# The gate of the residual folded into w_o on GpSimd, and the expert gathers taken from the unscaled rows

## The chip, the cores and the metric

One Trainium2 chip; the kernel runs on one of its cores. The time is the device time of one execution in microseconds (us). Before the change three executions took 749.11 us in the median (748.03 to 749.79). The engines: PE multiplies matrices (PEld is its loading of the stationary operand), DVE and ACT work on rows of 128 partitions, POOL is GpSimd, SP issues nearly all the transfers from HBM.

## The reference

One transformer layer on 256 tokens of 1024 channels in float32. What matters here is its second half:

```python
x = x + g1 * _mixer_out(...)          # _mixer_out ends in matmul(merged, w_o)
x = x + g2 * _hier_moe(_rmsnorm(x, norm2_g) * (1 + sc2) + sh2, ...)
# _hier_moe: top-1 of 4 groups, top-2 of the 8 experts in it, 32 experts of 1024 -> 512 -> 1024
for e in range(N_EXPERTS):
    hid = silu(t @ w1[e]) * (t @ w3[e])
    out = out + combine[:, e:e + 1] * (hid @ w2[e])
```

The gate `g1` is one number per output channel, so `g1 * (m @ w_o)` equals `m @ (w_o * g1)`. The root of `_rmsnorm` is one number per token.

## The kernel before

The mixer comes first, about 300 us. Each float32 weight is split on the way into a high part (ACT, `highs`) and the rest (DVE, `lows`, of the loaded tile `ld` and `highs`), half a tile (128x1024) at a time, and PE multiplies in three passes. PE, ACT and DVE work through a list written out by hand (`WORK`, lines 54 to 60): `s o 3` starts the split of half 3 of `w_o` on ACT, `l o 3` finishes it on DVE, `o k` and `N b k` are the matmuls of the output projection, `m` is a step of the modulation vectors on DVE (`macc`). While `run(WORK)` records, each of the three engines keeps the order of the list; POOL is outside of it and keeps the order in which its own instructions were scheduled.

Near the end of the list stand the steps that lead to the experts, for five pieces of the rows (`pieces2`): `ra` (line 1201) multiplies the product by the gate `gain(0)` on DVE, adds it to the row tile `xt()` and squares it on ACT; `rb` transposes on PE and copies on ACT; `rc` multiplies by the router weights; `rd` adds up sums of squares; `L t` makes the root of token tile `t` and its logits; `rt` chooses the experts; `pl` counts each token's place in its expert (`rank`). `rw` scales the rows by the root into a new tile `h2`, laid out as `(t, k, 128)`, and `ac` puts the rows into the accumulators `acc`.

After the list: `onehots(e)` (line 1301) compares places with slot numbers for four experts, so that `gather` (line 1316) can pull their tokens, transposed, by matmuls whose stationary operand is a 128x128 piece of `h2` and whose moving operand is the one-hot tile `oh`; DVE and ACT evict them with the modulation into `xg`. The experts go in 16 pairs: `hidden_mm` (line 1338) runs 8 rows `k` of w1 and w3 for two experts, `down` multiplies by w2, `scatter` adds into `acc`. For the first pair the second half of the gather stands at `k == 4` of `hidden_mm`.

The order of the transfers: about 20 buffers of 1 MB (lane `r`) hold weights. A planner (`plan_loads`) walks the recorded events of the program (a buffer taken, a buffer freed, a load first needed, a load done) and puts each load at the first event from which a buffer stays free. On the chip a load then waits in SP's queue until the last reader of the buffer it takes has ended. For the loads of this story: the buffers of the merged rows and of the splits are freed at step `hh` (line 1252), the buffer of the row tile at `done("x")` after the list, and the next ones by the first pair: `hidden_mm` declares its weights done after `k == 3` and after `k == 7`.

Of the kernel before, what the change touches and what calls it, by code (L numbers as in the profile page):

```python
# [10 lines left out]
I32 = mybir.dt.int32  # L11
# [118 lines left out]
def hybrid_block_kernel(  # L130
# [1005 lines left out]
    ss2 = sb(keep, [128, 2, 3], "ss2")  # L1136
    lg = sb(keep, [128, 2, 36], "lg")
# [99 lines left out]
    @step  # L1237
    def step_rd(p):
        t = pieces2[p][0]
        i = max(1, p - 2)  # L1240
        dve.tensor_tensor(out=ss2[:, t, 0:1], in0=ss2[:, t, 0:1], in1=ss2[:, t, i:i + 1], op=ALU.add)

    @step
    def step_L(t):

        r = banks["r2", t] = rstd_of(ss2[:, t, 0:1], D, f"rs2{t}")[0]
        dve.scalar_tensor_tensor(out=lg[:, t, :], in0=banks["lg", t][:, 0:36], scalar=r, in1=lb, op0=ALU.mult, op1=ALU.add)
        release(banks["lg", t])
# [8 lines left out]
    @step  # L1257
    def step_rw(t, n):

        act.activation(out=ready["h2"][:, t].rearrange("q k p -> q p k")[:, 64 * n:64 * n + 64],  # L1260
                       in_=xt()[:, t, 512 * n:512 * n + 512].rearrange("q (p k) -> q p k", k=KT), func=AF.Copy,
                       scale=banks["r2", t])
# [14 lines left out]
    rk_ps, h2 = banks["rk"], ready["h2"]  # L1277
# [3 lines left out]
    done("x")  # L1281
    for t in range(2):
        pe.matmul(rk_ps[0:1, 64:96], ones[:, 0:1], selm[:, t].rearrange("p g e -> p (g e)"), start=(t == 0), stop=(t == 1))
    cnt = sb(keep, [1, 1], "cnt")
    dve.tensor_reduce(out=cnt, in_=rk_ps[0:1, 64:96], axis=AX.X, op=ALU.max)
    cnt_i = sb(keep, [1, 1 + NE], "cnt_i", I32)
    dve.tensor_copy(out=cnt_i[:, 0:1], in_=cnt)
    dve.tensor_copy(out=cnt_i[:, 1:1 + NE], in_=rk_ps[0:1, 64:96])
    release(rk_ps)


    free_h, free_y = [free_m.pop(0)], [free_p.pop(0)]
    free_m.append(free_p.pop(0))
    while len(free_m) > 2:
        free_p.append(free_m.pop())
# [5 lines left out]
    def onehots(e):  # L1301
# [14 lines left out]
    def gather(kps=range(4), behind=None):  # L1316

        for kp in kps:
            ps = bank("xg_ps")
            pv = ps[:, 0:8 * CAP].rearrange("p (k n) -> p k n", k=2)  # L1320
# [6 lines left out]
            if kp % 2:  # L1327
                for kk in range(2):
                    act.activation(out=xg[:, kp, kk], in_=pv[:, kk], func=AF.Identity, scale=am2[:, 1, 2 * kp + kk:2 * kp + kk + 1],  # L1329
                                   bias=sh2[:, 1, 2 * kp + kk:2 * kp + kk + 1])  # L1330
            else:
                for kk in range(2):
                    k = 2 * kp + kk
                    mark["xg"] = dve.tensor_scalar(out=xg[:, kp, kk], in0=pv[:, kk], scalar1=am2[:, 1, k:k + 1],  # L1334
                                                   scalar2=sh2[:, 1, k:k + 1], op0=ALU.mult, op1=ALU.add)
# [87 lines left out]
    for p in range(NP):  # L1423
        hp = hidden_mm(lambda e, k: xg[:, k // 2, k % 2, CAP * (2 * (p % 2) + e):CAP * (2 * (p % 2) + e) + CAP],
                       *loaded_of(p), None if p else lambda: gather((2, 3)))
# [7 lines left out]
        if p % 2 and p + 1 < NP:  # L1433
# [7 lines left out]

    if events is not None:
# [60 lines left out]
    with tc.If(n_max > CAP):  # L1503
        for (t, n), a in acc.items():
            act.copy(out=xs[:, t, 512 * n:512 * n + 512], in_=a)
        with tc.For_i(0, NE, 1) as ei:
            n_own = nc.values_load(cnt_i[0:1, bass.ds(ei + 1, 1)], min_val=0, max_val=T)
            with tc.If(n_own > CAP):
# [136 lines left out]
```

## Time and profile before

| | before |
|---|---|
| median of three runs | 749.11 us (748.03 to 749.79) |
| the profiled execution | 747.63 us, its span 745.9 us |
| PE busy, DVE, ACT, POOL | 647.3, 289.4, 206.2, 9.9 us |
| moved from HBM | 265.66 MB read, 358 GB/s over the span |
| chain that ended last | DMA 51%, PE 45%, DVE 2%, ACT 1% |

The span has two parts. Up to about 310 us PE is busy nearly all the time and the chain of waits runs through it. From there the chain is the transfers of the experts' weights (192 MB), one after another, until 732 us. The row `PE 7999...` of the page shows the first part, `GB/s` (420 to 422 in nearly every slice of the second half) the second.

### The profile page before, as it was taken

Reading aid. Unit: us, or ns where it says so; the run is one execution under the profiler, and the core shown is the slowest. Engines: PE = TensorE matmul, PEld = TensorE weight load, DVE = VectorE, ACT = ScalarE, POOL = GpSimd, SP = SyncE. Lnnn points to the kernel's source line nnn. Section 1 sums busy time; section 2 is a strip of 40 time slices with the busy share of each in tenths; the row PEclk is TensorE's granted clock in tenths of the full one; section 3 lists DMA queues with packets and bytes.
Section 4 is the critical chain, followed back from the end, with each engine's and each line's share of the span. In section 5 each row is a group of like instructions: output and inputs, shape, how many; then the busy total and the mean of one; then the engine's idle time right before and its main releaser. Section 6 shows DMA issues by size and latency. Waiting matters only on the chain.

```text
span 745.9 us, 9959 instructions
## 1 busy us (share of the span) xinstructions
PE 647.3 (87%) x4050; PEld 367.8 (49%) x4051; DVE 289.4 (39%) x584; ACT 206.2 (28%) x387; POOL 9.9 (1%) x19
## 2 busy tenths in 40 slices
PE   7999999999999999899978867878977886887663
PEld 6789978879999988443313212222311321221110
DVE  4577986798676677421201200200200120020002
ACT  3345755786555566310000000000100000000012
POOL 0000000010000000000000000000000000000000
PEclk9999999999999999999989999989998999999997
DMA  9997542479998899999999999999999999999993
GB/s 319 362 397 302 196 151 71 133 271 365 350 352 296 322 339 345 360 422 421 420 422 421 421 422 420 420 422 421 421 420 422 421 421 422 420 421 422 420 421 146
DMA packets 55609, 267.43 MB, mean 359 GB/s; under 512 B 4612, under 2 KB 13572, under 8 KB 28804
## 3 DMA queue, kind: packets, MB, share of 16 engines
q1 hardware_dynamic: 54610, 266.19, 89.8%
q8 instruction: 34, 0.56, 0.3%
q10 hardware_dynamic: 948, 0.55, 0.2%
q14 instruction: 17, 0.14, 0.0%
HBM read 265.66 MB, written 1.05 MB: 358 GB/s over the span
## 4 chain that ended last, share of the span: by engine, by line
DMA 51%; PE 45%; DVE 2%; ACT 1%; issue 1%; SPq 0%; DVEq 0%; ACTq 0%
DMA ld<-in_moe_w_dram 50%; PE v L158 6%; PE hp L1347 4%; PE k L158 3%; PE Y L158 3%; PE wo L158 3%; PE g L158 2%; PE u L158 2%; PE q L158 2%; PE U L158 2%; PE V L158 2%; PE X L158 2%; PE T L158 2%; PE W L158 2%; PE G L158 1%; PE s_ps L158 1%
## 5 line engine op out<-in xcount | busy, mean ns | idle before, releaser
L1347 PE MATMUL hp<-ld,bc 128*32 128x512 f32 x1024 | 197.2, 641 | 47.0 <-DMA ld<-in_moe_w_dram 46.9
L1347 PEld LDWEIGHTS hp<-ld,bc 128*32 128x32 f32 x1024 | 40.9, 116 | 170.1 <-DMA ld<-in_moe_w_dram 90.9
L1381 PE MATMUL yp<-ld,wk 128*32 128x512 f32 x512 | 85.0, 600 | 18.1 <-DMA ld<-in_moe_w_dram 18.1
L1361 DVE COPY wk<-hp 128x256 f32<-128x256 f32 x16 | 6.7, 421 | 145.5 <-ACT wk L1360 145.5
L158 DVE TENSOR_TENSOR lows<-ld,highs 128x1024 fp32r<-128x1024 f32 x46 | 56.1, 1221 | 14.4 <-ACT highs L158 14.3
L158 ACT CAST highs<-ld 128x1024 fp32r<-128x1024 f32 x46 | 48.2, 1053 | 32.3 <-DMA ld<-in_w_in_dram 9.2
L1360 ACT COPY wk<-hp 128x256 f32<-128x256 f32 x16 | 5.9, 369 | 174.8 <-PE hp L1347 174.8
L1329 ACT ACTIVATE bc<-xg_ps,mcol 128x128 f32<-128x128 f32 x32 | 14.2, 457 | 125.1 <-PE hp L1347 114.2
L1381 PEld LDWEIGHTS yp<-ld,wk 128*32 128x32 f32 x512 | 17.2, 109 | 63.6 <-DMA ld<-in_moe_w_dram 39.0
L1323 PEld LDWEIGHTS xg_ps<-wr,h 128*128 128x128 f32 x256 | 31.4, 191 | 30.2 <-issue 26.0
L1334 DVE TENSOR_SCALAR bc<-xg_ps,mcol 128x128 f32<-128x128 f32 x32 | 12.8, 409 | 81.6 <-PE hp L1347 77.0
L1386 DVE TENSOR_TENSOR yb<-yp,bc 128x512 f32<-128x512 f32 x16 | 11.1, 692 | 82.9 <-PE yp L1381 82.9
L1403 PE MATMUL acc<-yb,wk 64*128 64x512 f32 x128 | 31.8, 615 | 11.1 <-DVE yb L1386 11.1
L158 DVE SCALAR_TENSOR_TENSOR macc<-ld,sj,macc 128x1024 f32<-128x1024 f32 x32 | 40.3, 1278 | 0.0
L1323 PE MATMUL xg_ps<-wr,h 128*128 128x128 f32 x256 | 38.6, 290 | 0.0
L1368 ACT ACTIVATE wk<-hT 128x256 f32<-128x256 f32 x16 | 6.2, 384 | 97.0 <-PE yp L1381 89.0
L1403 PEld LDWEIGHTS acc<-yb,wk 64*128 64x128 f32 x128 | 11.0, 186 | 32.3 <-DVE yb L1386 23.8
L158 ACT ACTIVATE gx<-gx 128x256 f32<-128x256 f32 (+2 forms) x56 | 24.8, 484 | 4.7 <-DVE gx L158 3.7
L158 PE MATMUL wo<-highs,ot 128*128 128x512 f32 (+1 forms) x80 | 20.0, 354 | 0.0
L158 PE MATMUL Y<-ot,highs 128*128 128x256 f32 x128 | 18.3, 285 | 0.0
L1312 DVE TENSOR_TENSOR yb<-cst,rank 128x128 f32<-128x128 f32 x32 | 9.0, 288 | 23.0 <-PE woT L1393 19.6
L1365 PE MATMUL hT<-cst,wk 128*128 128x128 f32 x64 | 12.9, 294 | 4.6 <-ACT wk L1360 4.0
(319 smaller groups left out, 913.0 us busy)
## 6 DMA issues: line engine op xcount, KB each, us to landing
ld<-in_moe_w_dram SPq DMA_DIRECT2D x191, 1024.0 KB, 19.8
ld<-in_w_mod_dram SPq DMA_DIRECT2D x24, 1024.0 KB, 5.3
ld<-in_w_in_dram SPq DMA_DIRECT2D x22, 1024.0 KB, 8.2
ld<-in_w_o_dram SPq DMA_DIRECT2D x4, 1024.0 KB, 8.4
ld<-in_w_gla_br_dram SPq DMA_DIRECT2D x4, 1024.0 KB, 10.1
ld<-in_w_pool_br_dram SPq DMA_DIRECT2D x2, 1024.0 KB
ld<-in_xT_dram SPq DMA_DIRECT2D x1, 1024.0 KB
ld<-in_cT_dram SPq DMA_DIRECT2D x1, 1024.0 KB
```

Source lines behind the costliest of these rows:

```text
L158: i = f(*args, **kwargs)
L1312: dve.tensor_tensor(out=wo, in0=slots_of[:, None, None, :].to_broadcast([128, 2, 2, CAP]), in1=rank[:, t, None, es, None].to_broadcast([12 ...
L1323: i = pe.matmul(pv[:, kk, :], h2[:, t, 2 * kp + kk, :], oh[:, t].rearrange("p e s -> p (e s)"), start=(t == 0), stop=(t == 1))
L1329: act.activation(out=xg[:, kp, kk], in_=pv[:, kk], func=AF.Identity, scale=am2[:, 1, 2 * kp + kk:2 * kp + kk + 1], bias=sh2[:, 1, 2 * kp + ...
L1334: mark["xg"] = dve.tensor_scalar(out=xg[:, kp, kk], in0=pv[:, kk], scalar1=am2[:, 1, k:k + 1], scalar2=sh2[:, 1, k:k + 1], op0=ALU.mult, o ...
L1347: mark["hp"] = pe.matmul(hp[o:o + CAP, :], xs(e, k), w[:, 512 * (k % 4):512 * (k % 4) + 512], start=(k == 0), stop=(k == KT - 1), tile_pos ...
L1361: dve.tensor_copy(out=hs[:, 2:4], in_=hv[:, 2:4])
L1365: pe.transpose(out=tp[:, 128 * k:128 * k + 128], in_=hs[:, k, :], identity=ident)
L1368: last_silu[:] = [act.activation(out=hid, in_=tv[:, :, 0, :], func=AF.Silu)]
L1381: pe.matmul(yp[r:r + CAP, :], hid[:, 2 * k + e, :], w[:, o:o + 512], start=(k == 0), stop=(k == 3), tile_position=(0, r))
L1386: dve.tensor_tensor(out=yb, in0=yp, in1=g2bc[:, 0:512], op=ALU.mult)
L1403: pe.matmul(acc[t, n], wT[rs, 128 * t:128 * t + 128], yb[rs, :], start=start, stop=stop, tile_position=(64 * n, 0))
```

## The change

The gate is multiplied into the halves of `w_o` on POOL, where `half_of` hands them to the split, in place; `ra` then adds the product straight to the rows. The sums of squares of both token tiles are reduced at once and one root is made for both. `rb` copies its last two pieces on DVE. There is no `h2`: `gather` reads the row tile itself, in steps of 8 elements (`xk`), and the root goes into the one-hots. The first gathers and their one-hots are made for two experts at a time, the second gather of the first pair stands at `k == 2`, and experts 2 and 3 are gathered after the first pair's `hidden_mm`. The row tile stays held to the end (`event("done", ...)`), so that buffer is not freed after the list; `h2` takes none.

```diff
-    N 2 4, ra 1, N 2 5, N 0 6, rb 0, N 0 7, sr 2, N 1 6, ra 2, N 1 7, N 2 6, rb 1, ra 3, N 2 7, rc 0, rb 2, rb 3, rc 1,
-    ra 4, rd 2, rd 4, rb 4, rc 2, rc 3, rc 4, hh, rd 3, ac 0 0, L 0, L 1, ac 1 0, ac 1 1, rt, rw 1 1, rw 0 0, pl,
-    ac 0 1, rw 0 1, rw 1 0"""
+    N 2 4, ra 1, N 2 5, N 0 6, rb 0, N 0 7, sr 2, N 1 6, ra 2, N 1 7, N 2 6, rb 1, ra 3, N 2 7, rc 0, rb 2, ra 4, rc 1,
+    rb 3, rb 4, rc 2, rd, rc 3, rc 4, hh, L, ac 0 0, ac 1 0, ac 1 1, rt, pl, ac 0 1"""
...
+        if kind == "o":
+
+            w, c0 = t[:, 1024 * i:1024 * i + 1024].rearrange("p (k n) -> p k n", k=2), 512 * (j // 4)
+            pool.tensor_tensor(out=w, in0=w, in1=gain(0)[:, None, c0:c0 + 512].to_broadcast([128, 2, 512]), op=ALU.mult)
...
+        dve.tensor_tensor(out=xt()[:, t, ns], in0=xt()[:, t, ns], in1=a[:, 0:m], op=ALU.add)
+        release(a)
+        i = (0, 0, 1, 1, 2)[p]
         tmp = sg_tile() if m == 512 else hid_tile()
-        dve.tensor_tensor(out=tmp, in0=a[:, 0:m], in1=gain(0)[:, ns], op=ALU.mult)
-        release(a)
-        dve.tensor_tensor(out=xt()[:, t, ns], in0=xt()[:, t, ns], in1=tmp, op=ALU.add)
-        i = (0, 0, 1, 1, 2)[p]
...
-        act.copy(out=banks["h", p], in_=tp[:, 0:m])
+        (dve.tensor_copy if p > 2 else act.copy)(out=banks["h", p], in_=tp[:, 0:m])
...
+    def step_rd():
+
+        ss = sb(keep, [128, 2], "ssr")
+        dve.tensor_reduce(out=ss, in_=ss2, axis=AX.X, op=ALU.add)
+        banks["r2"] = rstd_of(ss, D, "rs2")[0]
...
-        ready["h2"] = slot("h2", (2, KT, 128))
...
+    xk = xt().rearrange("q t (p k) -> q t k p", k=KT)
...
-    done("x")
...
+    def onehots(e, n=4, o=0):
 
         for t in range(2):
-            dve.tensor_tensor(out=oh[:, t], in0=slots_of[:, None, :].to_broadcast([128, 4, CAP]),
-                              in1=rank[:, t, e:e + 4, None].to_broadcast([128, 4, CAP]), op=ALU.is_equal)
+            for i in range(n):
+                mark["oh"] = dve.tensor_scalar(out=oh[:, t, o + i], in0=slots_of, scalar1=rank[:, t, e + i:e + i + 1],
+                                               scalar2=r2[:, t:t + 1], op0=ALU.is_equal, op1=ALU.mult)
...
-                    i = pe.matmul(pv[:, kk, :], h2[:, t, 2 * kp + kk, :], oh[:, t].rearrange("p e s -> p (e s)"),
-                                  start=(t == 0), stop=(t == 1))
+                    i = mark["first"] = pe.matmul(pv[:, kk, :], xk[:, t, 2 * kp + kk, :],
+                                                  oh[:, t, o:o + n].rearrange("p e s -> p (e s)"), start=(t == 0), stop=(t == 1))
...
-            if k == 4 and middle is not None:
+            if k == 2 and middle is not None:
...
-        onehots(0)
-    gather((0, 1))
+        onehots(0, 2)
+    gather((0, 1), None, 2)
...
-                       *loaded_of(p), None if p else lambda: gather((2, 3)))
+                       *loaded_of(p), None if p else lambda: gather((2, 3), None, 2))
...
-        if p % 2 and p + 1 < NP:
+        if p == 0:
+            onehots(2, 2, 2)
+            gather(range(4), mark["hp"], 2, 2)
+        elif p % 2 and p + 1 < NP:
```

How the instructions stand on three engines. PE around the first pair, before (`xg_ps` are gathers, `hp` the hidden matmuls, `rk` the counts, `acc` the rows into the accumulators):

```order
L158 MATMUL acc<-ld,cst 128x512 x3
L158 MATMUL rk<-selm,cst 128x64
L158 MATMUL rk<-selm,ones 128x32
L158 MATMUL acc<-ld,cst 128x512
L1283 MATMUL rk<-selm,ones 1x32 x2
L1323 MATMUL xg_ps<-wr,h_2807 128x128 x8
L1347 MATMUL hp<-ld,bc 32x512 x16
L1323 MATMUL xg_ps<-wr,h_2807 128x128 x8
L1347 MATMUL hp<-ld,bc 32x512 x16
L1365 MATMUL hT<-cst,wk 128x128 x4
```

and PE in the same place of the changed kernel:

```order
L157 MATMUL acc<-ld,cst 128x512
L1312 MATMUL xg_ps<-wr,ld 128x64 x8
L1397 MATMUL rk<-selm,ones 1x32 x2
L1335 MATMUL hp<-ld,bc 32x512 x8
L1312 MATMUL xg_ps<-wr,ld 128x64 x8
L1335 MATMUL hp<-ld,bc 32x512 x24
L1312 MATMUL xg_ps<-wr,ld 128x64 x16
L1335 MATMUL hp<-ld,bc 32x512
L1353 MATMUL hT<-cst,wk 128x128 x4
```

The count moved behind the first gather, the second gather moved ahead of half of the first 16 hidden matmuls, and 16 gathers more stand behind the pair.

POOL from its second `macc` on, before (`dec` are copies of one element):

```order
L823 MEMSET gy 128x512 x2
L859 COPY dec<-gx 128x1 x3
L1043 MEMSET macc 128x2048
L859 COPY dec<-gx 128x1
L1500 TENSOR_LOAD cnt_i
```

and in the changed kernel:

```order
L826 MEMSET gy 128x512 x2
L862 COPY dec<-gx 128x1 x3
L1046 MEMSET macc 128x2048
L862 COPY dec<-gx 128x1
L626 ISA
L626 TENSOR_TENSOR ld<-ld,bc 128x1024 x8
L1503 TENSOR_LOAD cnt_i
```

The eight products of `w_o` by the gate stand behind the last of those copies and ahead of nothing else that the mixer waits for.

DVE between the last pieces of `ra` and the logits, before (`wk` holds the gated product, `ss` sums of squares, `rs` roots):

```order
L158 TENSOR_TENSOR wk<-wo,bc 128x256
L158 TENSOR_TENSOR ld<-ld,wk 128x256
L158 TENSOR_TENSOR ss_128<-ss_128 128x1 x3
L158 TENSOR_SCALAR rs20m<-ss_128 128x1
L158 TENSOR_TENSOR rs20q<-rs_2811 128x1
L158 TENSOR_TENSOR rs20q<-rs20q,rs20m 128x1
L158 SCALAR_TENSOR_TENSOR rs_2811<-rs20q,rs_2811 128x1
L158 SCALAR_TENSOR_TENSOR lg<-lg,rs_2811,lb 128x36
L158 TENSOR_SCALAR rs21m<-ss_128 128x1
```

and in the changed kernel:

```order
L157 TENSOR_TENSOR ld<-ld,wo 128x256 x2
L157 COPY wk<-h2T 128x256 x2
L157 TENSOR_REDUCE ssr<-ss_128 128x2
L157 TENSOR_SCALAR rs2m<-ssr 128x2
L157 TENSOR_TENSOR rs2q<-rs_2801 128x2
L157 TENSOR_TENSOR rs2q<-rs2q,rs2m 128x2
L157 SCALAR_TENSOR_TENSOR rs_2801<-rs2q,rs_2801 128x2
L157 SCALAR_TENSOR_TENSOR lg<-lg,rs_2801,lb 128x36 x2
```

One sum, one chain of four instructions for the root and two logits in a row stand where two chains stood, and the two copies of transposed pieces are new on DVE.

## Rows read from the trace of the kernel before

**Rows 1.** Windows: each engine's busy us (instructions), granted clock, DMA share, GB/s.
```profile
165.00:187.00 22.00, 21.09 (x171) 19.26 (x170) 18.38 (x32) 14.84 (x27) 0.00 (x0) 1.00 0.94 342
216.00:236.00 20.00, 20.00 (x170) 20.00 (x169) 15.42 (x21) 9.64 (x15) 0.00 (x0) 1.00 0.87 318
...
300.00:306.00 6.00, 6.00 (x50) 3.02 (x53) 4.48 (x35) 1.49 (x7) 0.00 (x0) 1.00 0.95 343
306.00:312.00 6.00, 6.00 (x56) 2.80 (x48) 1.39 (x6) 0.81 (x2) 0.00 (x0) 1.00 0.80 300
312.00:352.00 40.00, 39.03 (x300) 15.45 (x300) 10.55 (x34) 5.17 (x11) 0.00 (x0) 1.00 1.01 422
352.00:732.00 380.00, 301.06 (x1616) 87.20 (x1608) 46.76 (x134) 21.44 (x51) 0.00 (x0) 0.96 1.01 420
```

**Rows 2.** Waits of SP's queue, 225 to 312 us: total us, times, longest us.
```profile
SPq L311 <- PE hp L1347: 5.4, 1, 5.4
```

**Rows 3.** Timeline of SP's queue: start us, us, what was issued.
```profile
306.68 2.04 SPq L311 DMA_DIRECT2D ld<-in_moe_w_dram  x4
```

**Rows 4.** The chain that ended last, 299 to 307 us: start us, us, what.
```profile
299.33 0.63 PE rk L158 x4
299.97 0.94 PE acc L158 x2
300.91 0.21 PE rk L1283 x4
301.12 1.98 PE xg_ps L1323 x16
303.10 3.57 PE hp L1347 x32
```

**Rows 5.** PEld by form, 285 to 345 us: busy us, mean ns, idle before.
```profile
L1323 PEld LDWEIGHTS xg_ps<-wr,h 128*128 128x128 f32 x66 | 7.7, 191 | 2.6 <-issue 2.5
...
L158 PEld LDWEIGHTS lg<-wr,wk 128*128 128x128 f32 x32 | 3.8, 192 | 0.0
```

**Rows 6.** Timeline of DVE, the logits of the two token tiles.
```profile
295.50 0.26 DVE L158 SCALAR_TENSOR_TENSOR lg<-lg,rs,lb 128x36 f32<-128x36 f32 x1
...
296.38 0.26 DVE L158 SCALAR_TENSOR_TENSOR lg<-lg,rs,lb 128x36 f32<-128x36 f32 x1
```

**Rows 7.** Timeline of SP's queue, the four loads of w_o.
```profile
155.97 0.47 SPq L313 DMA_DIRECT2D ld<-in_w_o_dram  x1
...
171.91 0.37 SPq L313 DMA_DIRECT2D ld<-in_w_o_dram  x1
...
209.08 0.46 SPq L313 DMA_DIRECT2D ld<-in_w_o_dram  x1
...
214.34 0.37 SPq L313 DMA_DIRECT2D ld<-in_w_o_dram  x1
```

**Rows 8.** Timeline of POOL, four copies of one element and a memset.
```profile
91.17 0.80 POOL L859 COPY dec<-gx 128x1 f32<-128x1 f32 x1 [5.41 <-ACT gx L158]
...
113.21 0.18 POOL L859 COPY dec<-gx 128x1 f32<-128x1 f32 x1 [9.56 <-ACT gx L158]
...
153.76 1.01 POOL L859 COPY dec<-gx 128x1 f32<-128x1 f32 x1 [10.98 <-ACT gx L158]
155.99 1.81 POOL L1043 MEMSET macc<- 128x2048 f32 x1 [1.21 <-DVE macc L158]
164.49 0.41 POOL L859 COPY dec<-gx 128x1 f32<-128x1 f32 x1 [6.69 <-ACT gx L158]
```

**Rows 9.** Timeline of DVE beside those copies.
```profile
90.70 1.22 DVE L158 TENSOR_TENSOR lows<-ld,highs 128x1024 fp32r<-128x1024 f32 x1
...
153.45 1.28 DVE L158 SCALAR_TENSOR_TENSOR macc<-ld,sj,macc 128x1024 f32<-128x1024 f32 x1
```

**Rows 10.** ACT by form, 285 to 301 us: busy us, mean ns, idle before.
```profile
L158 ACT ACTIVATE h<-ld,rs 128x512 f32<-128x512 f32 x4 | 4.0, 1143 | 1.1 <-DVE rs L158 1.1
L158 ACT ACTIVATE wk<-ld 128x512 f32<-128x512 f32 x3 | 1.9, 632 | 2.3 <-DVE ld L158 2.3
```

More of the change, by code (lines that the diff above doesn't have):

```diff
@@ L1136, in hybrid_block_kernel @@
     ss2 = sb(keep, [128, 2, 3], "ss2")
+    pool.memset(ss2, 0.0)
     lg = sb(keep, [128, 2, 36], "lg")
@@ L1237, in step_rd, with step_L @@
     @step
[L1238 to L1241, printed above, removed]
+    def step_rd():
+        ss = sb(keep, [128, 2], "ssr")
+        dve.tensor_reduce(out=ss, in_=ss2, axis=AX.X, op=ALU.add)
+        banks["r2"] = rstd_of(ss, D, "rs2")[0]
     @step
[L1244 to L1248, printed above, removed]
+    def step_L():
+        for t in range(2):
+            dve.scalar_tensor_tensor(out=lg[:, t, :], in0=banks["lg", t][:, 0:36], scalar=banks["r2"][:, t:t + 1], in1=lb,
+                                     op0=ALU.mult, op1=ALU.add)
+            release(banks["lg", t])
     @step
@@ L1254, in step_hh @@
         move(2, "w", "r")
-        ready["h2"] = slot("h2", (2, KT, 128))
[L1257 to L1262, printed above, removed]
     @step
@@ L1276, in hybrid_block_kernel @@
     run(WORK)
-    rk_ps, h2 = banks["rk"], ready["h2"]
+    rk_ps, r2 = banks["rk"], banks["r2"]
+    xk = xt().rearrange("q t (p k) -> q t k p", k=KT)
     g1bc, g2bc = gain(0), gain(1)
@@ L1280, in hybrid_block_kernel @@
     move(1, "w", "r")
-    done("x")
[L1282 to L1295, printed above, removed]
+    free_h, free_y = [free_m.pop(0)], []
+    while len(free_m) < 2:
+        free_m.append(free_p.pop(0))
     xg = g1bc.rearrange("p (i j s) -> p i j s", i=4, j=2)
@@ L1299, in hybrid_block_kernel @@
     slots_of = slot64[:, 0:CAP]
-    def onehots(e):
+    def onehots(e, n=4, o=0):
         for t in range(2):
-            dve.tensor_tensor(out=oh[:, t], in0=slots_of[:, None, :].to_broadcast([128, 4, CAP]),
-                              in1=rank[:, t, e:e + 4, None].to_broadcast([128, 4, CAP]), op=ALU.is_equal)
+            for i in range(n):
+                mark["oh"] = dve.tensor_scalar(out=oh[:, t, o + i], in0=slots_of, scalar1=rank[:, t, e + i:e + i + 1],
+                                               scalar2=r2[:, t:t + 1], op0=ALU.is_equal, op1=ALU.mult)
     def weighted(p):
@@ L1314, in weighted, with gather @@
             dve.tensor_tensor(out=wo, in0=wo, in1=cf[:, None, es, None].to_broadcast([128, 2, 2, CAP]), op=ALU.mult)
-    def gather(kps=range(4), behind=None):
+    def gather(kps=range(4), behind=None, n=4, o=0):
+        cs = slice(CAP * o, CAP * (o + n))
         for kp in kps:
             ps = bank("xg_ps")
-            pv = ps[:, 0:8 * CAP].rearrange("p (k n) -> p k n", k=2)
+            pv = ps[:, 0:2 * n * CAP].rearrange("p (k n) -> p k n", k=2)
             for kk in range(2):
                 for t in range(2):
-                    i = pe.matmul(pv[:, kk, :], h2[:, t, 2 * kp + kk, :], oh[:, t].rearrange("p e s -> p (e s)"),
-                                  start=(t == 0), stop=(t == 1))
+                    i = mark["first"] = pe.matmul(pv[:, kk, :], xk[:, t, 2 * kp + kk, :],
+                                                  oh[:, t, o:o + n].rearrange("p e s -> p (e s)"), start=(t == 0), stop=(t == 1))
                     if behind is not None:
                         after(i, behind)
[L1327 to L1334, printed above, removed]
+            for kk in range(2):
+                k = 2 * kp + kk
+                if kp % 2:
+                    act.activation(out=xg[:, kp, kk, cs], in_=pv[:, kk], func=AF.Identity, scale=am2[:, 1, k:k + 1],
+                                   bias=sh2[:, 1, k:k + 1])
+                else:
+                    mark["xg"] = dve.tensor_scalar(out=xg[:, kp, kk, cs], in0=pv[:, kk], scalar1=am2[:, 1, k:k + 1],
                                                    scalar2=sh2[:, 1, k:k + 1], op0=ALU.mult, op1=ALU.add)
@@ L1405, in hybrid_block_kernel @@
     with tc.high_priority():
-        onehots(0)
-    gather((0, 1))
+        onehots(0, 2)
+    gather((0, 1), None, 2)
+    for t in range(2):
+        i = pe.matmul(rk_ps[0:1, 64:96], ones[:, 0:1], selm[:, t].rearrange("p g e -> p (g e)"), start=(t == 0), stop=(t == 1))
+        after(i, mark["first"])
+    cnt = sb(keep, [1, 1], "cnt")
+    dve.tensor_reduce(out=cnt, in_=rk_ps[0:1, 64:96], axis=AX.X, op=ALU.max)
+    cnt_i = sb(keep, [1, 1 + NE], "cnt_i", I32)
+    dve.tensor_copy(out=cnt_i[:, 0:1], in_=cnt)
+    dve.tensor_copy(out=cnt_i[:, 1:1 + NE], in_=rk_ps[0:1, 64:96])
+    release(rk_ps)
+    free_y.append(free_p.pop(0))
     for t in range(2):
@@ L1440, in hybrid_block_kernel @@
     finish(NP - 1, hid)
+    event("done", index("x"))
     if events is not None:
@@ L1521, in hybrid_block_kernel @@
                         dve.tensor_scalar(out=oh[:, t, 0:2].rearrange("p e s -> p (e s)"), in0=slot64, scalar1=rc[:, t],
-                                          scalar2=None, op0=ALU.is_equal)
+                                          scalar2=r2[:, t:t + 1], op0=ALU.is_equal, op1=ALU.mult)
                         for i in range(2):
@@ L1528, in hybrid_block_kernel @@
                         for t in range(2):
-                            pe.matmul(ps[:, two * k:two * k + two], h2[:, t, k, :], oh[:, t, 0:2].rearrange("p e s -> p (e s)"),
+                            pe.matmul(ps[:, two * k:two * k + two], xk[:, t, k, :], oh[:, t, 0:2].rearrange("p e s -> p (e s)"),
                                       start=(t == 0), stop=(t == 1))
```

## Prediction

> **What bounds the kernel now.** I read the windows first, then SP's waits, then the chain. From 312 us on the transfers run at 422 GB/s with no gap, while PE is busy 301 of 380 us [rows 1]: there the end is a matter of bytes, and work added to PE, DVE or ACT costs nothing. Just before it the stream has a hole: 343 GB/s from 300 to 306 and 300 from 306 to 312 [rows 1]. Against 422 that is (79 x 6 + 122 x 6) / 422 = 2.9 us, all that an earlier start of the experts could give back. SP names what makes the hole: it waited 5.4 us in one piece for PE's hidden matmuls [rows 2] and issued four loads at 306.68 [rows 3]. The chain has the same instant: gathers from 301.12 for 1.98 us, then 16 hidden matmuls (each is two rows of PE) for 3.57, so 306.67 [rows 4]. That block frees the first four buffers. So one instant, the end of the first 16 hidden matmuls, decides the end of the kernel, and whatever moves it moves the end by as much, up to 2.9 us for a gain and without a limit for a loss. Before it everything hangs on PE: where the products of w_o would run (165 to 187 and 216 to 236 us) PE was busy 21.09 of 22 and 20.00 of 20 us and DVE 18.38 and 15.42 [rows 1]. A delay that reaches PE there passes to the end in full.
>
> **The first pair.** Before, from the first gather to the decisive instant: 1.98 + 3.57 = 5.55 us [rows 4]. After, the second gather stands inside the first 16 hidden matmuls, so both gathers precede the instant. Does a gather of 64 columns cost half of one of 128? The loads of the stationary operand took 7.7 us / 66 = 0.117 us each for the gathers with 128 moving columns and 3.8 / 32 = 0.119 for the router's matmuls with 36 [rows 5]. They stand back to back, so the load sets the pace and the number of columns does nothing. Eight gathers (16 loads) of two experts cost 16 x 0.117 = 1.87 us. The sum after is 1.87 + 0.21 (the count, now behind the gather [rows 4]) + 3.57 + 1.87 = 7.52, which is 1.97 longer.
>
> Against this the start comes sooner. The count's 0.21 us no longer stands ahead of it. One root instead of two chains: the logits of the second tile began at 296.38, those of the first at 295.50 [rows 6]; if both go at the first one's time, 0.8 is saved. But the one sum now waits for the squares of all pieces and on DVE behind two new copies, so I take 0.5 (0 to 0.9). The one-hots become more and smaller instructions; PE has a matmul of the accumulators of 0.94 us to do between the ranks and the gather [rows 4], which hides them. The adds of `ra` (one instruction fewer per piece) lie beside the output projection and the router, PE's work. Scaling the rows (`rw`, four ACT instructions, 4.0 us [rows 10]) lay beside the routing on DVE, so leaving it out gives nothing. So the instant moves by 1.97 - 0.7 = **+1.2 us** (0.8 to 1.8). The two loads that may now be issued sooner (the buffer that `h2` took, and that of the split work space) end before the same hole; the next load waits for the same instant. The other 16 gathers of the first pair, and one-hots of eight instructions for two, come behind it, in PE's 79 spare microseconds.
>
> **The products on POOL.** Eight of 128x1024, two per loaded tile. The tiles were issued at 155.97, 171.91, 209.08 and 214.34 [rows 7]; POOL gets to them after its last copy at 164.49 [rows 8]. So four run in the first window and four in the second, 40 us and more before the output projection needs them: their own time is hidden. What they do to DVE is not. POOL's copies of a single element took 0.18 us at best, but 0.80, 1.01 and 0.41 elsewhere [rows 8]. The one of 91.17 ended at 91.97, the DVE instruction with two operands in SBUF that began at 90.70 ended at 91.92; that of 153.76 ended at 154.77, DVE's of 153.45 at 154.73 [rows 8, 9]. So a POOL instruction that reads waits until such a DVE instruction has ended. I take this exclusion as mutual: the `lows` and `macc` steps of DVE would then wait for a whole POOL product. The Trainium skill (SBUF — State Buffer, "Who interferes with whom") says it so: the pair is an exclusive lock held for a whole instruction, and a DVE instruction with two SBUF inputs contends with a GpSimd one that reads. By that rule the trace's half agrees, and the other half no row shows, since a copy of one element holds nothing for long.
>
> How long is one product? Nothing in the trace shows it. POOL wrote 2048 elements in 1.81 us [rows 8], 0.91 for 1024. One pass would be 0.9 us, two reads and a write in turn 2.7; I take two reads in turn, 1.9, since the write can go beside them. The same page set (GPSIMD Engine Reference, "Performance versus the Vector engine") has 4497 ns for 2048 elements; the estimate from it is 2.25 for ours, and the term below would be 9.8.
>
> The term: in the first window four products hold 7.6 us and DVE had 22 - 18.38 = 3.6 idle, so 4.0 run over; in the second 7.6 against 20 - 15.42 = 4.6, so 3.0 [rows 1]. Sum **+7.0 us** on PE, which has no idle time to take it up. Two things are left out that pull in opposite directions: DVE's idle time is partly waiting for ACT and can't all be used, and its `macc` steps aren't urgent. The ends: at 0.9 us a product fits into the idle time (0 us); at 2.7 it is 7.2 + 6.2 = 13.4; and 0 if DVE doesn't wait for POOL at all. It can't be below zero, since no work of DVE in these windows is taken away.
>
> **Sum.** +1.2 + 7.0 = +8.2 us. The profiled execution was 747.63, so it would be 755.8. The median shown is 749.11, 1.5 higher, so I predict **757.3**; the rivals are given on the same footing. About 0.2%, 1.5 us, is what a measurement here can tell from no change.
>
> **Rivals.**
> - *Strided weights are slow.* The gathers' stationary operand now comes from the row tile in steps of 8 elements (32 bytes), before it was dense. The nearest row is ACT writing `h2` in steps: 1.143 us for 512 columns, against 0.632 for the same count dense [rows 10], a factor of 1.8. The 32 loads ahead of the instant would go from 0.117 to 0.21 to 0.23 us, +3.0 to +3.7: 761.0 with the lock, 754.0 without. Against it: that row is a write by another engine with a step of 512 bytes, and no PE row reads with a step. The Trainium skill (Advanced Engine Details and Errata, "Memory Cachelines") speaks against the change: lines of 16 bytes, and a penalty where each access goes to another line; it gives no size, and by it this rival would hold.
> - *POOL does not hold DVE up* (it yields, or its reads pass between DVE's). For it: rows show only POOL waiting. Then +1.2 alone, 750.3, no change that can be told.
> - *Faster.* If a gather with 64 columns did cost half (0.94 for eight instead of 1.87), the path would be 0.94 + 0.21 + 3.57 + 0.94 = 5.66, 0.1 longer than before, from a start 0.7 to 1.1 earlier: -0.6 to -1.0, and with every other term at its best end about -1.5, so 747.6 to 748.5, and only with POOL harmless. It decides where eight gathers take under (5.55 + 0.7 - 3.57 - 0.21) / 2 = 1.24 us. Against it the equal loads with 36 and 128 columns [rows 5].
>
> **Chances.** The lock with dense-speed weights, 757.3: 0.38. The lock and slow strided weights, 761.0: 0.26. Slow weights without the lock, 754.0: 0.12. Neither, 750.3: 0.17. Faster: 0.07. The likeliest one's own range is 752 to 762. The range over all, 749.8 to 762.8, leaves out the faster case, the lower part of "neither" and the top of a 2.7 us product. Slower by over 0.2% (above 750.6): the first three and a quarter of the fourth, 0.80; within 0.2%: the rest of it and some of the last, 0.15; faster: 0.05.
>
> **What would show it.** The lock: `lows` and `macc` rows of DVE between 165 and 236 us longer than their 1.22 and 1.28, or gaps ahead of them named after POOL, products of about 1.9 us on POOL, idle time on PE in both windows, and the output projection starting some 7 us later than 266. Where POOL's rows stretch and DVE's don't, POOL is the one that yields. The first pair: 16 `xg_ps` rows of PE in 1.9 us for 64 columns (0.9 would be the faster rival, 3.5 the strided one), and SP's four loads 7.5 us after the first gather instead of 5.6. The hole in the stream: as deep as before or deeper, and 420 GB/s behind it. I'd be wrong if the output projection starts as before and the hole closes.

## The result and the profile after

| | before | after |
|---|---|---|
| median of the runs | 748.67 us (748.03 to 749.79, 4 runs) | 770.27 us (769.88 to 770.75, 4 runs) |
| profiled execution, its span | 747.63, 745.9 us | 770.75, 769.0 us |
| granted clock, mean | 0.972 | 0.960 |

The ratio is 1.029, with a 95% interval of 1.0279 to 1.0302: 21.6 us slower, where 8.2 were forecast. The windows of the changed kernel, in the columns of [rows 1]:

```profile
165.00:187.00 22.00, 16.22 (x127) 13.66 (x125) 21.05 (x27) 13.87 (x25) 12.00 (x5) 1.00 0.79 286
216.00:236.00 20.00, 20.00 (x168) 19.80 (x166) 18.77 (x18) 11.33 (x15) 10.21 (x4) 1.00 0.87 324
300.00:306.00 6.00, 6.00 (x54) 5.76 (x53) 2.63 (x11) 3.21 (x10) 0.00 (x0) 1.00 0.78 277
306.00:312.00 6.00, 5.26 (x18) 2.92 (x17) 4.53 (x30) 0.00 (x0) 0.00 (x0) 0.96 1.01 426
312.00:352.00 40.00, 40.00 (x212) 23.42 (x213) 11.05 (x61) 5.79 (x16) 0.00 (x0) 0.75 0.66 263
352.00:732.00 380.00, 328.13 (x1724) 119.37 (x1723) 59.01 (x186) 22.16 (x55) 0.00 (x0) 0.97 1.01 421
```

Behind 352 us nothing has changed: 421 GB/s. The loss lies in two places. In the mixer, PE is busy 16.22 of 22 us where it was 21.09, and POOL is busy 12.00 where it did nothing. From 312 to 352 us the stream moves 263 GB/s where it moved 422, with PE busy all the time and its granted clock at 0.75. The same stretch in pieces of 4 us shows two holes, not one:

```profile
312.00:316.00 4.00, 4.00 (x23) 3.03 (x27) 1.64 (x14) 0.98 (x5) 0.00 (x0) 0.50 0.86 358
316.00:320.00 4.00, 4.00 (x20) 2.00 (x12) 1.27 (x14) 0.30 (x3) 0.00 (x0) 0.71 0.02 8
320.00:324.00 4.00, 4.00 (x22) 2.57 (x25) 2.27 (x14) 0.70 (x2) 0.00 (x0) 0.71 0.00 0
324.00:328.00 4.00, 4.00 (x40) 1.10 (x36) 0.00 (x0) 0.00 (x0) 0.00 (x0) 0.86 0.37 84
...
340.00:344.00 4.00, 4.00 (x32) 0.96 (x28) 0.42 (x1) 0.12 (x1) 0.00 (x0) 0.73 0.52 219
344.00:348.00 4.00, 4.00 (x39) 0.99 (x31) 0.00 (x0) 0.00 (x0) 0.00 (x0) 1.00 0.81 266
```

Against 421 GB/s the first lacks (63 + 413 + 421 + 337) x 4 / 421 = 11.7 us, the second (202 + 155) x 4 / 421 = 3.4. Before there was one of 2.9. With the first gather 9.45 us later (310.57 against 301.12) that makes 9.45 + 11.7 + 3.4 - 2.9 = 21.65 us of the 23.1 by which the two profiled spans differ; the medians differ by 21.6.

SP's waits and issues say where the holes end (columns as in [rows 2, 3]), first its longest wait:

```profile
SPq L310 <- PE hp L1335: 49.4, 26, 19.6
```

```profile
325.60 2.05 SPq L310 DMA_DIRECT2D ld<-in_moe_w_dram  x4
...
343.73 0.33 SPq L310 DMA_DIRECT2D ld<-in_moe_w_dram  x1
```

The four loads that went out at 306.68 [rows 3] go out at 325.60, 15.03 us after the first gather instead of 5.56; SP waited 19.6 us for PE's hidden matmuls, not 5.4. The chain of waits (columns as in [rows 4]):

```profile
276.60 5.68 PE wo L157 x24
...
310.57 4.04 PE xg_ps L1312 x16
...
318.33 3.99 PE xg_ps L1312 x16
322.32 6.69 PE hp L1335 x48
329.01 7.80 PE xg_ps L1312 x32
...
347.95 4.00 PE xg_ps L1312 x16
```

The output projection starts at 276.60, 10 us later than before (266.61). A group of eight gathers (16 records) takes 4.0 us where it took 1.98, at whatever place. The weight loads show why (PEld by form, 308 to 318 us; columns as in [rows 5]):

```profile
L1312 PEld LDWEIGHTS xg_ps<-wr,ld 128*128 128x128 f32 x16 | 3.9, 334 | 0.8 <-issue 0.8
```

3.9 / 16 = 0.24 us for a load; before 0.117.

In the mixer, POOL's eight products (timeline, columns as in [rows 8]):

```profile
166.38 6.13 POOL L626 TENSOR_TENSOR ld<-ld,bc 128x1024 f32<-128x1024 f32 x2 [1.29 <-ACT bc L157]
181.05 5.78 POOL L626 TENSOR_TENSOR ld<-ld,bc 128x1024 f32<-128x1024 f32 x2 [8.54 <-ACT highs L157]
...
225.79 12.54 POOL L626 TENSOR_TENSOR ld<-ld,bc 128x1024 f32<-128x1024 f32 x4 [38.95 <-DMA ld<-in_w_o_dram]
```

and VectorE beside them (columns as in [rows 9]):

```profile
168.60 1.69 DVE L157 TENSOR_TENSOR gy<-gy 128x256 f32<-128x256 f32 x1
170.22 3.38 DVE L157 TENSOR_TENSOR lows<-ld,highs 128x1024 fp32r<-128x1024 f32 x1
...
177.77 0.29 DVE L157 CAST yp<-wk 128x256 fp32r<-128x256 f32 x1
178.09 0.43 DVE L157 TENSOR_TENSOR yp<-wk,yp 128x256 fp32r<-128x256 f32 x1
...
182.49 2.14 DVE L157 CAST yp<-wk 128x256 fp32r<-128x256 f32 x1 [0.25 <-ACT wk L157]
184.66 2.46 DVE L157 TENSOR_TENSOR yp<-wk,yp 128x256 fp32r<-128x256 f32 x1
...
226.24 3.15 DVE L157 SCALAR_TENSOR_TENSOR lows<-ld,cols,highs 128x1024 fp32r<-128x1024 f32 x1 [0.20 <-ACT highs L157]
...
230.04 6.03 DVE L157 SCALAR_TENSOR_TENSOR lows<-ld,cols,highs 128x1024 fp32r<-128x1024 f32 x2
```

The same `yp` step takes 0.43 us without a product beside it and 2.46 with one; `lows` takes 3.38 instead of 1.22. Each stretched instruction is 1.3 to 2.2 us too long. PE then waits for exactly these (waits of PE, 165 to 245 us: total, times, longest):

```profile
PE W L157 <- DVE yp L157: 3.6, 3, 1.7
PE kr_ps L157 <- DVE gz L157: 1.4, 1, 1.4
PE V L157 <- DVE lows L157: 1.3, 1, 1.3
```

The first two lines, 5.0 us, stand ahead of T's matmuls (those that write tile `T`, the next long step of the list), the third belongs to the second window. T's matmuls start at 201.7 us, before at 193.9. Behind the waits the granted clock fell as well (windows of the changed kernel):

```profile
188.00:190.00 2.00, 2.00 (x14) 2.00 (x13) 2.00 (x2) 0.00 (x0) 0.00 (x0) 0.65 0.09 33
190.00:192.00 2.00, 2.00 (x8) 1.73 (x7) 1.31 (x2) 0.00 (x0) 0.00 (x0) 0.50 0.47 78
```

From the last of these waits to T's first matmul, in the changed kernel and then in one of the experiments below with the same mixer (the step of 8 bytes), where the clock stayed at 1.00:

```profile
187.17 0.74 PE L157 MATMUL W<-yp,highs 128*128 128x256 f32 x4 [1.75 <-DVE yp L157]
...
201.69 1.30 PE L157 MATMUL T<-hx,highs 128*128 128x256 f32 x8
```

```profile
186.78 0.74 PE L158 MATMUL W<-yp,highs 128*128 128x256 f32 x4 [1.75 <-DVE yp L158]
...
199.74 1.30 PE L158 MATMUL T<-hx,highs 128*128 128x256 f32 x8
```

That is 14.52 us against 12.96, so 1.6 of the 7.8 us are the clock's.

### The profile page after: what moved, and what is told of

Its sections match the earlier page's. It is cut to its first block, busy times and chain, and to the rows that moved or that the text cites. A ratio compares the mean times of both kernels' runs of the same rounds, so it can differ in the third digit from the quotient of the medians.

```text
span 769.0 us, 10077 instructions
## 1 busy us (share of the span) xinstructions
PE 686.1 (89%) x4082; PEld 409.1 (53%) x4083; DVE 311.4 (40%) x627; ACT 202.5 (26%) x383; POOL 34.3 (4%) x28
## 4 chain that ended last, share of the span: by engine, by line
DMA 53%; PE 39%; DVE 4%; SPq 1%; issue 1%; ACT 0%; POOL 0%; DVEq 0%
DMA ld<-in_moe_w_dram 51%; PE v L157 6%; PE xg_ps L1312 3%; PE k L157 3%; PE hp L1335 3%; PE wo L157 3%; PE Y L157 3%; DMA ld<-in_w_mod_dram 2%; PE U L157 1%; PE X L157 1%; PE T L157 1%; PE g L157 1%; PE V L157 1%; PE o_ps L157 1%; PE u L157 1%; PE q L157 1%
## 5 line engine op out<-in xcount | busy, mean ns | idle before, releaser
L1369 PE MATMUL yp<-ld,wk 128*32 128x512 f32 x512 | 83.2, 601 | 14.9 <-DMA ld<-in_moe_w_dram 14.7
L1312 PEld LDWEIGHTS xg_ps<-wr,ld 128*128 128x128 f32 x288 | 71.6, 332 | 33.5 <-issue 29.3
L1312 PE MATMUL xg_ps<-wr,ld 128*128 128x128 f32 (+1 forms) x288 | 79.0, 420 | 0.0
L157 DVE TENSOR_TENSOR lows<-ld,highs 128x1024 fp32r<-128x1024 f32 x46 | 58.3, 1269 | 12.8 <-ACT highs L157 12.7
L1319 ACT ACTIVATE bc<-xg_ps,mcol 128x128 f32<-128x128 f32 (+1 forms) x36 | 15.4, 444 | 146.1 <-PE hp L1335 116.1
L1322 DVE TENSOR_SCALAR bc<-xg_ps,mcol 128x128 f32<-128x128 f32 (+1 forms) x36 | 13.8, 394 | 78.1 <-PE hp L1335 64.0
L1292 DVE TENSOR_SCALAR wr<-cst,rank,rs 128x32 f32<-128x32 f32 x64 | 14.7, 297 | 32.1 <-PE xg_ps L1312 32.0
L626 POOL TENSOR_TENSOR ld<-ld,bc 128x1024 f32<-128x1024 f32 x8 | 24.5, 3080 | 48.8 <-DMA ld<-in_w_o_dram 39.0
```

What stands on the lines that cost most here:

```text
L157: i = f(*args, **kwargs)
L626: pool.tensor_tensor(out=w, in0=w, in1=gain(0)[:, None, c0:c0 + 512].to_broadcast([128, 2, 512]), op=ALU.mult)
L1292: mark["oh"] = dve.tensor_scalar(out=oh[:, t, o + i], in0=slots_of, scalar1=rank[:, t, e + i:e + i + 1], scalar2=r2[:, t:t + 1], op0=ALU.i ...
L1312: i = mark["first"] = pe.matmul(pv[:, kk, :], xk[:, t, 2 * kp + kk, :], oh[:, t, o:o + n].rearrange("p e s -> p (e s)"), start=(t == 0), s ...
L1319: act.activation(out=xg[:, kp, kk, cs], in_=pv[:, kk], func=AF.Identity, scale=am2[:, 1, k:k + 1], bias=sh2[:, 1, k:k + 1])
L1322: mark["xg"] = dve.tensor_scalar(out=xg[:, kp, kk, cs], in0=pv[:, kk], scalar1=am2[:, 1, k:k + 1], scalar2=sh2[:, 1, k:k + 1], op0=ALU.mul ...
```

## The experiments

Theory: three parts add up. The products and VectorE hold each other up (some 10 us); the weights with a 32-byte step load slowly (some 10); the place of the gathers costs the rest.

**Without the products.** In `half_of` the four lines of the product go, and `ra` multiplies again (`...` marks what is left out):

```diff
-            pool.tensor_tensor(out=w, in0=w, in1=gain(0)[:, None, c0:c0 + 512].to_broadcast([128, 2, 512]), op=ALU.mult)
...
+        dve.tensor_tensor(out=tmp, in0=a[:, 0:m], in1=gain(0)[:, ns], op=ALU.mult)
...
```

> The changed kernel without its eight products on GpSimd: the gate is multiplied in on VectorE after the output projection, as in the kernel before; the rest of the change stays. Theory (three additive parts: the products and VectorE hold each other up, about 10 us; the strided weights of the gathers and what follows them, about 9; the place of the gathers, 1 to 3): about 760.5 us, and T's matmuls start near 194 us again instead of 202. Rival (the mixer's ten microseconds come from something else, or are hidden by the hole that follows): over 766 us. Second rival (the holes in the stream are there because the mixer ends late): under 755 us.

Measured: 760.93 us (759.30 to 761.54), 9.3 less than the changed kernel. `lows` is back at 1.22 and 1.28 us throughout, and T's matmuls start at 195.0 us. The first hole stays (the four loads go out 14.76 us after the first gather).

**The products alone**, in the kernel before (the same two edits the other way round).

> The kernel before with the eight products on GpSimd and nothing else of the change (the residual then only adds). Theory: 758 to 759 us, since the ten microseconds in the mixer reach the end in full and the residual gives back half of one; VectorE's lows beside a product take 2.5 to 3.5 us instead of 1.2. Rival (GpSimd delays nobody by itself, the delay needs the rest of the change): within 1 us of 748.7. Forecast of the prediction by itself: plus 7, 755.7.

Measured: 758.77 us, ratio 1.0134 (1.0113 to 1.0155), 10.8 over the 747.99 of before on the same chip. From both sides the products cost 9 to 11 us.

**Gathers from a dense copy**, in the changed kernel. The copy takes a buffer again, and that of the row tile is freed after the list, as before the change:

```diff
+        act.copy(out=ready["h2"][:, t].rearrange("q k p -> q p k")[:, 64 * n:64 * n + 64],
+                 in_=xt()[:, t, 512 * n:512 * n + 512].rearrange("q (p k) -> q p k", k=KT))
...
-    xk = xt().rearrange("q t (p k) -> q t k p", k=KT)
+    xk = ready["h2"]
...
```

> The changed kernel, but the gathers read a dense copy of the rows, which ScalarE writes as before (four copies, without the root, which stays in the one-hots). Theory (the 32-byte step of the weights costs 2.1 times the load): a group of 16 gather records takes 2.0 us instead of 4.0, the first hole loses 4 to 6 us, the second most of its 3.4; 761 to 763 us. Rival (the granted clock of 1.2 GHz in this stretch slows the gathers, not the step): the records still take over 3 us and the time stays over 767 us. Second rival (only the first two gathers count): 766 us.

Measured: 760.42 us (759.23 to 761.73), 9.9 less than the changed kernel. PE's timeline (start us, us, records):

```profile
310.24 1.97 PE L1321 MATMUL xg_ps<-wr,h 128*128 128x64 f32 x16
...
312.26 1.88 PE L1344 MATMUL hp<-ld,bc 128*32 128x512 f32 x13
314.07 2.00 PE L1321 MATMUL xg_ps<-wr,h 128*128 128x64 f32 x16
```

The gather takes 1.97 us, the loads go out 7.69 us after it starts (at 317.93), the second hole is gone, and the granted clock is 1.00 in all windows. Step and clock went together here, so this run alone doesn't part them.

**The second gather behind the first 16 hidden matmuls**, in the changed kernel:

```diff
-            if k == 2 and middle is not None:
+            if k == 4 and middle is not None:
```

> The changed kernel, but the second gather of the first pair stands behind the first 16 hidden matmuls, where it stood before, not behind the first 8. Theory (the end of the first 16 hidden matmuls alone sets the first hole): one gather of 4.0 us leaves that path, 766 to 767 us. Rival (the end of the first pair and of the gather behind it set a second hole, which takes over what the first gives back): 769 to 771 us, with the second hole 3 to 4 us deeper.

Measured: 767.43 us (764.25 to 768.86), 2.8 less, between the two forecasts. The loads go out 9.26 us after the first gather instead of 15.03, but only half of these 5.8 us reach the end. The second hole takes the rest:

```profile
336.00:340.00 4.00, 4.00 (x16) 1.37 (x19) 1.89 (x8) 2.37 (x4) 0.00 (x0) 0.57 0.42 176
340.00:344.00 4.00, 4.00 (x40) 1.08 (x36) 0.10 (x1) 0.00 (x0) 0.00 (x0) 1.00 0.24 37
```

Its deficit is (245 + 384) x 4 / 421 = 6.0 us where it was 3.4, so 5.8 - 2.6 = 3.2 should be left. So the end of the first pair with the 16 slow gathers behind it is a second instant that decides.

**Only the place of the gathers** (both edits undone), and then **that without the early second gather**, and then **by four experts**. The last two are:

```diff
+            if k == 4 and middle is not None:          # second and third kernel
...
-        onehots(0, 2)                                  # third kernel
-    gather((0, 1), None, 2)
+        onehots(0)
+    gather((0, 1))
...
```

> The changed kernel with both of the edits above undone: the gate on VectorE, the gathers from a dense copy. What is left of the change is the place of the gathers (by two experts, the second behind the first 8 hidden matmuls, 16 more behind the first pair), one root for both token tiles and the count behind the first gather. Theory (the parts add): 770.3 less 9.4 less 9.9, 751.0 us, with a first hole of 4 to 5 us in the stream instead of 2.9. Rival (products and stride fed the same hole, so that taking both away gives back less than the sum): 753 to 756 us. Second rival (the one root and the later count win more than the place loses): under 748 us.

> The same, and the second gather behind the first 16 hidden matmuls as in the kernel before. Theory: the path to the end of the first 16 hidden matmuls is that of before, 5.5 us, and starts 0.7 us earlier; the gather of the other two experts then stands behind the first pair beside a full stream: 748 to 749 us, 2 us less than without this. Rival (the 16 gathers behind the first pair make the second hole by themselves): as before this edit, within 0.5 us of it.

> The same, and the first gathers by four experts, so that nothing but the one root, the root in the one-hots, the count behind the first gather and the two copies on VectorE is left of the change. Theory: a gather of 128 columns costs what one of 64 does, so the path does not grow, and the 16 gathers behind the first pair are gone: 747.5 to 748.5 us, 0.3 to 1 us under the kernel before. Rival (the eight one-hot instructions, where before there were two, stand ahead of the first gather and eat the 0.7 us): 748.5 to 750 us.

Measured: 751.33, 748.93 and 749.63 us beside 748.38 of before; ratios 1.0040 (1.0026 to 1.0053), 1.0005 (0.9997 to 1.0014) and 1.0008 (1.0000 to 1.0017). The parts add: 9.3 + 9.9 + 2.9 = 22.1 against 21.6; the kernel before came to 747.99 to 748.67 us beside these runs, so such sums are good to some 0.7 us. The early second gather costs 2.4 us; the 16 dense gathers behind the first pair cost nothing. The third kernel met its rival: its first gather waited 0.43 us for the one-hots; its output projection also began 1.6 us later than before (268.1 against 266.5), which no row explains. No version beats the kernel before by more than a measurement can tell.

**One operand instead of two on POOL**, in the kernel before, eight and sixteen times:

```diff
+            pool.tensor_scalar(out=w, in0=w, scalar1=1.0, scalar2=None, op0=ALU.mult)
```

> The kernel before, with eight GpSimd instructions on the same tiles of the output projection's weights, in the same places, but with one operand: each multiplies its half by 1.0, so that the result is that of before and only the second operand is missing against the products. Theory (any GpSimd instruction that reads SBUF and VectorE's instructions hold each other up, in its whole length): the copies take 1.5 to 2.2 us each, VectorE's lows beside them 2 us or more, and the time grows in proportion to their length, to 753 to 756 us. Rival (only a GpSimd instruction with two operands takes what VectorE needs): VectorE's lows stay at 1.2 us and the time within 1 us of 748.5.

> The kernel before with sixteen one-operand GpSimd instructions (each half of the output projection's weights multiplied by 1.0 twice) where eight were. Eight held VectorE some 0.8 us each (lows 2.09 us where 1.22 are usual) and cost 0.6 us in the end; eight products held it some 2 us each and cost 10. Theory (the sum of the held time decides, whatever the operands): 16 x 0.8 = 13 us held, near the products' 16, so 4 to 8 us over the kernel before, 753 to 757 us. Rival (one-operand instructions fit between VectorE's own and cost next to nothing however many): within 1.5 us of 749.2.

Measured: 749.23 us (ratio 1.0008, 0.9998 to 1.0018) and 751.38 (1.0045, 1.0029 to 1.0060). POOL and VectorE in the kernel with eight:

```profile
166.24 7.94 POOL L626 TENSOR_SCALAR ld<-ld 128x1024 f32<-128x1024 f32 x2 [7.26 <-DMA ld<-in_w_o_dram]
```

```profile
169.94 1.22 DVE L158 TENSOR_TENSOR lows<-ld,highs 128x1024 fp32r<-128x1024 f32 x1
171.08 0.48 DVE L158 CAST yp<-wk 128x256 fp32r<-128x256 f32 x1
171.59 1.13 DVE L158 TENSOR_TENSOR yp<-wk,yp 128x256 fp32r<-128x256 f32 x1
...
179.48 2.09 DVE L158 TENSOR_TENSOR lows<-ld,highs 128x1024 fp32r<-128x1024 f32 x1 [0.46 <-ACT highs L158]
```

POOL's instruction looks even longer than a product (7.94 us for two), but each VectorE instruction is held by 0.2 to 0.9 us only; that the rest is POOL waiting is likely, but no row shows it. So the length of a POOL row is not what it takes from VectorE. Of the forecasts for eight, the time came out as the rival's, the longest `lows` as the theory's. This execution, 750.82 us, is one of the slower ones: its output projection starts at 269.2, 2.7 us later than before. Both forecasts for sixteen missed, one by too much (753 to 757), one by too little: it came to 3.3 us. Whether the second operand matters beyond the shorter hold stays open.

**The products on VectorE itself**, in the kernel before (`dve` for `pool` in that line).

> The kernel before with the eight products on VectorE itself, not on GpSimd. Eight times 1.22 us, the time of lows with the same two operands and 1024 elements, come to VectorE, 9.8 us, where GpSimd's products held it 8 x 2 us. Theory (VectorE's time is what the mixer is short of): between the two, 753 to 756 us. Rival (VectorE has room for them, it was the lock's bad moments that cost): within 2 us of before, 748 to 751 us.

Measured: 758.80 us, ratio 1.0138 (1.0121 to 1.0155), no better than POOL's 758.77 and worse than forecast. The mixer is not delayed (T's matmuls start at 194.3, before at 193.9), but each product now runs just ahead of the split that needs it, and PE waits in the output projection:

```profile
PE wo L158 <- ACT highs L158: 3.6, 5, 1.0
PE wo L158 <- DVE lows L158: 2.3, 4, 0.8
```

**The step or the clock.** Three kernels part the 9.9 us of the strided weights. Dense with every gather matmul issued twice; a copy in which the step is 8 bytes; and the changed kernel's strided loads, as many in the same places, but each with 128 columns:

```diff
-                for t in range(2):
+                for t in (0, 1, 0, 1):                 # twice
...
-    gather((0, 1), None, 2)                            # wide
+    gather((0, 1))
...
-            onehots(2, 2, 2)
-            gather(range(4), mark["hp"], 2, 2)
+            gather(range(4), mark["hp"])
```

> The changed kernel with the gathers from the dense copy (GpSimd's products stay), but each gather matmul of the rounds by pairs is issued twice, so that 32 dense loads stand where 16 were, as long as 16 loads with the 32-byte step. It tells the load time of the strided weights from the fall of the granted clock that came with them. Theory (time of the loads alone): the 32 records take 4.0 us, the granted clock stays 1.00, and the time is that of the changed kernel less what the clock cost it, 1 to 2 us: 768 to 769 us. Rival (any long run of gathers lets the clock fall): 0.5 to 0.9 in the windows of the first pair, and 770 us.

> The changed kernel with the gathers from a copy (GpSimd's products stay), but in the copy two rows' elements alternate, so that the weights of a gather have a step of 8 bytes, not 4 (dense) or 32 (the changed kernel). Theory (the price of a weight load grows with the step by degrees): 0.15 to 0.2 us for each load, 763 to 766 us. Rival (any step but 4 bytes costs the whole factor of 2.1): 0.25 us, 770 us. Second rival (only steps of 16 bytes and more cost): 0.12 us, 760.4 us.

> The changed kernel with as many strided gather loads in the same places, but each moves 128 columns (four experts) instead of 64: the first two gathers write all four experts, and the 16 behind the first pair write the same four once more, to no use. Theory (a strided load with 64 columns leaves TensorE so little to do that the granted clock falls to 1.2 GHz, and the fall is worth some 5 us beside the load time): 1.00 or near it in the windows of the first pair, hidden matmuls 0.11 us apart again instead of 0.22, 765 to 767 us (the first gather some 0.5 us later, since eight one-hots stand before it, not four). Rival (the stride itself lets the clock fall): 0.5 to 0.9 in these windows and 770 to 771 us.

Measured: 764.72, 759.08 and 767.03 us. Twice the dense loads cost 4.3 us over the dense copy, at a granted clock of 1.00 in every window of the first pair, so both forecasts for it were too high. A step of 8 bytes is all but free, 3.9 / 32 = 0.12 us a load:

```profile
L1324 PEld LDWEIGHTS xg_ps<-wr,h 128*128 128x128 f32 x32 | 3.9, 196 | 1.7 <-issue 1.7
```

The wide kernel decides on the clock. PE's timeline in it, and then the hidden matmuls of the changed kernel, between its gathers of 310.57 and 318.33:

```profile
311.93 4.04 PE L1312 MATMUL xg_ps<-wr,ld 128*128 128x128 f32 x16 [0.42 <-DVE wr L1292]
...
316.01 1.88 PE L1335 MATMUL hp<-ld,bc 128*32 128x512 f32 x13
317.83 4.08 PE L1312 MATMUL xg_ps<-wr,ld 128*128 128x128 f32 x16
```

```profile
314.73 3.60 PE L1335 MATMUL hp<-ld,bc 128*32 128x512 f32 x13
```

The gathers take the same 4.0 us, but the hidden matmuls behind them 1.88 instead of 3.60, and the granted clock reads 1.00 in every window of the stretch where it had fallen to 0.50 to 0.86. From the first gather to the loads' issue it is 11.84 us (311.93 to 323.77), against 15.03 with 64 columns and 7.69 dense. So of the 7.34 us by which the step lengthens that path, 4.15 are load time (32 x 0.13) and 3.19 the clock at its 1.2 GHz level.

The medians of these kernels carry something else too. All have the same products, but T's matmuls start between 199.7 us (8 bytes) and 204.5 (twice) in their profiled executions, with a granted clock of 1.00 to 0.81 from 187 to 205 us. So it is safer to count each span from its first gather to its end: 448.9 us dense, 447.8 with 8 bytes, 452.3 twice, 454.3 wide and 458.4 changed (before: 444.9). The step then costs 9.5 us: 5.4 of them come with the loads (dense to wide), 4.1 with the clock (wide to changed). The path of the first hole has 4.15 and 3.19 of these; the rest, 2.2, is left for the second hole. The windows give the same sum with another split: the first hole is 11.7 us against 5.5 in the dense kernel, the second 3.4 against none (1.9 in the wide one), 9.6 together. Twice the dense loads, without a fall of the clock, lengthened the path by 3.6 (11.27 us) and the end by 3.4.

## Why the prediction was wrong

**The direction was right, the size was not**, +21.6 against +8.2 us. By its steps:

- **"One instant ... decides the end".** Right for the first hole: in the experiments too the four loads go out at that instant. Incomplete behind it: with slow gathers the end of the first pair is a second such instant. "The other 16 gathers ... come behind it, in PE's 79 spare microseconds" holds for dense weights (748.93 with them, 749.63 without) and fails for strided ones. The 79 were counted behind 352 us; from 312 to 352, where these gathers stand, PE had been busy 39.03 of 40 us [rows 1].
- **The strided weights were put at nothing; this is the step that failed most.** The slow load was a rival with chances of 0.26 and 0.12, and its price, +3.0 to +3.7 for 32 loads, was near the 4.15 measured. But the sum took the other value because "no PE row reads with a step", and the rival counted load time alone. It left out that the hidden matmuls between the gathers would run at half the clock (3.2 us) and that 16 more slow gathers stand ahead of the next release (2.2). Together 9.5, or 9.9 by the medians. The Trainium skill (Advanced Engine Details and Errata, "Memory Cachelines") wants at least two hits on a 16-byte line for full speed; the runs agree: a step of 8 bytes took 0.12 us a load, one of 32 bytes 0.24. It was the rule that spoke against the change, and weighed too little.
- **The products: mechanism right, term mis-sized, +10.0 instead of +7.0.** The exclusion is mutual, as taken, and a product holds VectorE for 1.3 to 2.2 us where 1.9 were taken, though its row on POOL is 3.08 long, not the 1.9 that were to show it. But +4.0 and +3.0 came from letting VectorE's idle time swallow part of it. In the first window some 7.3 us were held, and 5.0 reached PE, because PE waits there for short `yp` and `gz` steps of VectorE in turn. Behind these waits the clock cost 1.6 more, for which the sum had no term; 1.2 of the 7.8 there no row names. In the second window 2.2 were lost instead of 3.0. In the seven profiled executions with products the second loss is 2.2 to 2.3 each time, the first between 5.8 and 10.6: in the two with 5.8 and 7.5 the clock stayed at 1.00, in the one with 10.6 it was lowest. The rule of the Trainium skill quoted there (SBUF — State Buffer, "Who interferes with whom": an exclusive lock for the whole instruction) agrees with the rows of the products, and with a cast with one SBUF operand too (2.14 us for 0.29).
- **The first pair's place.** That a gather of 64 columns costs as much as one of 128: right (1.97 and 2.05 us). The path of 7.52: 7.69 in both dense runs. The start 0.7 earlier: 0.5, by the distance from the start of the output projection in the run with only the place changed (300.36 - 266.3, against 301.05 - 266.5 in PE's timeline). The term +1.2 came out at 2.9 by the medians. 2.4 of it is the early second gather, worth 1.97 in the working; the earlier start gained nothing in time (748.93 against 748.38 with the path as before): from its first gather to its end that kernel takes 446.0 us, before it was 444.9. Why stays open.
- **The other edits at nothing** (one root, the root in the one-hots, the adds, no scaled rows): right within what a measurement can tell.

## What to carry to other kernels

Before the weights of a matmul are read with a step, look at how many loads stand on the path and at what runs between them: here a 32-byte step doubled each load, and in the kernel with 64 columns to a load, not in the one with 128, the clock fell for the matmuls in between as well. An engine's idle time in a window absorbs little of a lock where another engine waits for its short results in turn; here 5.0 of 7.3 us passed on, and the clock fell behind the waits. Where a part of the kernel varies from run to run, compare the rest from a common instant. And where an edit lengthens one release of buffers, look for the next release: it may take over what the first gives back.

## What the hardware did that was not expected

- A load of fp32 weights took 0.117 us dense, 0.12 with a step of 8 bytes and 0.24 with 32, whether 64 or 128 columns followed; the 0.24 at either clock.
- The granted clock fell to 0.50 (1.2 GHz) in the windows with strided gathers of 64 columns, while PE counted as busy throughout; with the same loads and 128 columns, or with twice as many dense loads of 64, it stayed at 1.00. In the mixer it fell to 0.50 behind PE's waits for VectorE in five of the seven profiled executions with products, and stayed at 1.00 in the other two.
- A VectorE cast with a single SBUF operand was held by a POOL product as much as an instruction with two (2.14 us for 0.29).
- A POOL instruction with one operand showed 3.17 us on average in its own row and held VectorE 0.2 to 0.9; a product showed 3.08 on average and held it 1.3 to 2.2.
